# A hybrid decoder layer on one core: gate's second K half multiplied first for all feature tiles, stored, and added later

## The chip, the core and the metric

One core of one Trainium2 chip computes the whole layer. Its engines work side by side: TensorE (PE) multiplies, VectorE (DVE) and ScalarE (ACT) do elementwise work, GpSimd (POOL) a little, and SyncE (SP) issues most transfers. The metric is the device time of one execution in microseconds. Before the change it was 1936.91 us, the median of 3 runs (1934.86 to 1938.24).

## The reference, cut to what matters

```python
x = x + 0.5 * swiglu_ffn(rmsnorm(x, ffn1_norm), ffn1_w_gate, ffn1_w_up, ffn1_w_down)
x = x + hybrid_mixer(rmsnorm(x, mix_norm), ...)
x = x + 0.5 * swiglu_ffn(rmsnorm(x, ffn2_norm), ffn2_w_gate, ffn2_w_up, ffn2_w_down)
return rmsnorm(x, final_norm)

def rmsnorm(x, g):                       # scale of a token: 1 / rms over its 1024 features
    y = x * lax.rsqrt(jnp.mean(x * x, axis=-1, keepdims=True) + EPS)
    return y * g
def swiglu_ffn(x, w_gate, w_up, w_down):
    return (jax.nn.silu(x @ w_gate) * (x @ w_up)) @ w_down
```

x is 1024 tokens by 1024 features in float32; the feed-forward width is 2816. The change touches only the two feed-forward blocks, and there only gate and up. The mixer between them (attention and gated linear attention) stays as it is.

## The kernel before, in words

Tokens lie as columns, features on the partitions. Every float32 operand is split in two parts, a high one by a copy on ACT and a low one, the remainder, by a subtraction on DVE. A product of two such operands is three matmuls (`mm3`, L192 to L194): high by high, high by low, low by high, 128 x 128 weights against 512 tokens.

Gate and up of a feed-forward block are done for 22 feature tiles of 128 (FT = 22). Call gate's two K halves of a tile A11 and A12, up's A21 and A22, and the tokens' quarters B11, B21 (first and second K half of the first 512 tokens) and B12, B22 (the same of the second 512). A *product* is one weight half against one token quarter: four 128-row weight blocks, 12 matmuls. A *plain* tile takes 8 products (`plain`). A tile by the seven-product scheme (`strassen`) takes 7: A11 x B11, A12 x B21, S1 x T1, S2 x T2, S3 x T3, S4 x B22, A22 x T4, where S1 to S4 are sums of weight halves (`sums`, L396) and T1 to T4 differences of token quarters (`combine`, L333 for the differences and L312 for their low parts). T's are made once a block, S's once a tile. So T1 to T4 must be there before the first such tile, and in each block some plain tiles come first: 4 (`std, rms_of = 4, [None]`) in block 1, 2 in block 2.

Block 1 begins with tokens that have only their gain (`lift`, L319 and L320): the token scale is not known yet, and the plain tiles' results of the first 512 tokens are multiplied by it afterwards (`rb`, L510 and L513). Meanwhile side work (`first`) finds the scale (squares on ACT, sums on DVE, a matmul with ones L267, a power on POOL, a broadcast by matmul L279), scales the tokens in place (L303, L1877), splits and combines them.

The order of the work is written out: the recording code makes PE's products one after the other, and after every three matmuls a clock (`tick`) lets the side work take one step. The steps are counted: `until(24)` and `t0 + k == 28` are numbers of such steps. Weights are copied and split a few products ahead (`LOOK = 4`), each engine works through its own queue in order, and an instruction that waits holds everything behind it on its engine. A tile's raw weights come as two 512 KB transfers on SP's queue (`load`), gate's into one of three `raw` buffers.

After a tile of the seven-product scheme four steps collect its banks: p1 copies bank X after A11 x B11 and p2 adds A12 x B21's own bank Z to it (L564), which gives gate for the first 512 tokens; p6 and p5 copy X after S2 and S1 (L541), and p5's second step adds bank Y (L573); p3 takes gate for the second 512 tokens, p4 up. A22 x T4 is accumulated on bank Y, so it waits for p5's addition. X and Y alternate between two pairs of banks.

Of the kernel before, what the change touches and what calls it, by code (L numbers as in the profile page):

```python
# [32 lines left out]
AHEAD2 = 12  # L33


class Layer:
# [256 lines left out]
    def normed(self, rb, x, h, which, half, inplace=False, pace=1):  # L293
# [4 lines left out]
        for k in range(KT + 2):  # L298
            if k > 1:
                lows.pop(0)()  # L300
            if k < KT:
                hf = x[:, k, ts] if inplace else self.nt.tile([128, 512], F32, name="hf")
                nc.vector.scalar_tensor_tensor(hf, x[:, k, ts], self.gains[:, which, k:k + 1], rb,  # L303
                                               op0=OP.mult, op1=OP.mult)
                lows.append(self.halve(h[half][k], hf))
            for _ in range(int((k + 1) * pace) - int(k * pace)):
                yield
# [6 lines left out]
    def lift(self, x, h, which, half, k):  # L314
# [3 lines left out]
        hi = h[half][k][:, 0]  # L318
        nc.scalar.activation(hi, xk, AF.Copy, scale=gain)  # L319
        nc.vector.scalar_tensor_tensor(h[half][k][:, 1], xk, gain, hi.bitcast(F32), op0=OP.mult, op1=OP.subtract)  # L320
# [8 lines left out]
    def combine(self, x, B, std, pace=1):  # L329
# [20 lines left out]
        for name, k0, ts in (("T2", 4, hi), ("T3", 0, hi), ("T1", 0, lo), ("T4", 4, lo)):  # L350
            while self.room("TA") < (5 if self.pos[0] >= 8 * std - 2 else 9):
                self.reserve = 4 * (self.pos[0] >= 8 * std)
                if lows:
                    lows.pop(0)()
                yield
# [15 lines left out]
    def ffn(self, w, B, rb, std, late, load, raws, hooks):  # L371
# [9 lines left out]
        tb = self.dram.tile([HK, 128, 2, 512], F32, name="tb")  # L381
        minus = lambda o, p, q: nc.vector.tensor_tensor(o, p, q, OP.subtract)
# [14 lines left out]

        def source(f, q):
            if q[0] == "S":
# [4 lines left out]
        def ready(f, q, kinds):  # L404
# [3 lines left out]
            if q == "A12" and f >= std:  # L408
# [5 lines left out]
            def low():  # L414
                nc.vector.tensor_tensor(t[:, 1], a, t[:, 0].bitcast(F32), OP.subtract)  # L415
                if q == "A11" and f >= std:
                    sums(f, 1)
                if q in ("S1", "S4"):
# [30 lines left out]
        def both(i, banks, post):  # L449
# [10 lines left out]
            for m in range(2):  # L460
                q = f"A{m + 1}{i + 1}"
                seq.append(((0, q), lambda kinds, q=q: ready(0, q, kinds), mm if m else lambda: None, post if m else None))

# [79 lines left out]
        def strassen(f):  # L543

            def pair():
                if f not in X:
                    X[f], Y[f] = [self.one_bank((f - FT) % 2 * 2 + i) for i in range(2)]
                    partner(f)
                return X[f]
# [21 lines left out]
            def p5():  # L571
                snap(G[0][:, 1], X[f])
                todo.append([0, lambda: nc.vector.tensor_tensor(G[0][:, 1], Y[f], G[0][:, 1], OP.add)])  # L573
# [167 lines left out]
        groups = {f: strassen(f) for f in range(std, FT)}  # L741
        for f in range(std, FT):
# [3 lines left out]
            groups[f][2]()  # L746
# [31 lines left out]
        def step(i=None):  # L778
# [3 lines left out]
            if make and key not in made:  # L782
# [10 lines left out]
                if key[1] in ("A11", "A12"):  # L793
# [8 lines left out]
        def go():  # L802
            for i, (key, _, mm, post) in enumerate(seq):
# [20 lines left out]
                if i == turn - 1:  # L824
                    self.free(*G)
            self.free(*S, *s2.values())
        return step, settle, go


# [941 lines left out]
    def run(self, ffn=True):  # L1771
# [16 lines left out]
        h = [[self.take("AT", "h") for _ in range(KT)] for _ in range(2)]  # L1788
# [26 lines left out]
        load_x(0, 0, 1)  # L1815
        one(w1, 0, 0, 0)
        load_x(0, 1, 1)
        one(w1, 0, 1, 0)
        load_x(0, 2)
        one(w1, 0, 0, 1)  # L1820
        load_x(0, 4)
        one(w1, 0, 1, 1)
        load_x(0, 6, 1)
        load_x(0, 7, 1)
        for m in range(2):
            one(w1, 1, m)
        self.load_consts()
        for k in range(0, KT, 2):
            load_x(1, k)
        ns, B = [{}, {}], {f"u{i + 1}{half + 1}": h[half][4 * i:4 * i + 4] for i in range(2) for half in range(1)}  # L1830
# [5 lines left out]
        def begin(step, settle):  # L1836
            for k in range(KT):
                self.lift(x, h, 0, 0, k)
                if k in (0, 1, 3, 5):
# [3 lines left out]
        def first(std):  # L1843
# [9 lines left out]
            for half, t0 in enumerate((0, 24)):  # L1853
                yield from until(t0)
                if half:
                    for _ in range(2):
                        next(rms[0])
                for k in range(KT):
                    if half and t0 + k == 28:
                        for _ in range(2):  # L1860
                            next(rms[0])
                    self.squares(ns[half], x, slice(half * 512, half * 512 + 512), k, nc.vector, "hf" if half else "acc")
                    yield from until(t0 + k + 1)
                    if half and t0 + k == 30:
                        nc.scalar.activation(rb[:, 0], ns[0]["rb"], AF.Copy)
                self.total(ns[half], nc.vector)
            yield from until(36)
            for _ in range(2):
                next(rms[1])
            yield from until(40)  # L1870
            for _ in range(2):
                next(rms[1])
            yield from until(41)
            yield from self.normed(ns[1]["rb"], x, h, 0, 1, True, 2.5)
            B["12"], B["22"] = h[1][:4], h[1][4:]
            for k in range(KT):
                nc.vector.scalar_tensor_tensor(x[:, k, :512], x[:, k, :512], self.gains[:, 0, k:k + 1], rb[:, 0],  # L1877
                                               op0=OP.mult, op1=OP.mult)
                yield
            while self.pos[0] < 4 * std:  # L1880
                yield
            lows = []
            for k in range(KT + 2):
                if k > 1:
                    lows.pop(0)()
                if k < KT:
                    lows.append(self.halve(h[0][k], x[:, k, :512]))
                if k in (5, 9):
                    B["21" if k > 5 else "11"] = h[0][k - 5:k - 1]
                yield  # L1890
            yield from self.combine(x, B, std)
            while self.pos[0] < 8 * std:
                yield
# [33 lines left out]
        def again(src):  # L1927
# [9 lines left out]
            def back():  # L1937
# [5 lines left out]
        std, rms_of = 4, [None]  # L1943
        self.open_banks(False)
        step, settle, go = self.ffn(w1, B, lambda: rms_of[0][:, 0], std, 5, loader(w1), raws,
                                    {"post": post, "x": again(ins["xT"]), (10, "A22"): self.round_consts,
                                     ("2", 3, 2): lambda: self.raws(0), ("3", 0): lambda: self.later(2),
                                     (std, "A11"): lambda: self.free(*B.pop("12"), rms_of[0])})
# [4 lines left out]
        self.side.append(first(std))  # L1953
# [11 lines left out]
        B, std = {}, 2  # L1965
        out = {}

        def second(x):
            for half in range(2):
# [9 lines left out]
                B[f"1{half + 1}"], B[f"2{half + 1}"] = hg[half][:4], hg[half][4:]  # L1979
            yield from self.combine(x, B, std)  # L1980
# [57 lines left out]
        def post2(ts, ot):  # L2038
# [9 lines left out]
            if ot == (3 if half else 7):  # L2048
# [3 lines left out]
        step, settle, go = self.ffn(w2, B, lambda: None, std, 1, loader(w2), raws,  # L2052
                            {"post": post2, "x": again(xs), "parts": (slice(0, 256), slice(256, 512)), (std, "A11"): lambda: self.free(*B.pop("12"))})
        for half in range(2):
            ts = slice(half * 512, half * 512 + 512)
            for i in range(2 * half, KT + 2 * half):
# [15 lines left out]
                if half and ot == 5:  # L2072
                    loader(w2)(0)
# [128 lines left out]
```

## Time and profile before

| quantity | value |
|---|---|
| median of the runs | 1936.91 us |
| span of the profiled execution | 1938.6 us |
| granted PE clock, mean | 0.997 |
| PE busy | 1922.5 us (99%) |
| DVE, ACT busy | 1334.0 us (69%), 862.1 us (44%) |
| moved by DMA | 292.47 MB, 151 GB/s |
| first matmul of block 1's weights | 5.63 us |
| first T product of block 1, of block 2 | 105.33 us, 1338.93 us |
| first product of block 2 | 1287.61 us |

The page has no time for the profiled execution beside its span; that span lies 0.4 us above the slowest of the three runs. A row of the timeline gives start, duration, engine, line, operation, output and inputs, and in brackets how long the engine stood idle before and what it waited for. Matmul durations overlap, so the spacing of their starts is what one costs.

### The profile page before, as it was taken

Reading aid. Unit: us, or ns where it says so; the run is one execution under the profiler, and the core shown is the slowest. Engines: PE = TensorE matmul, PEld = TensorE weight load, DVE = VectorE, ACT = ScalarE, POOL = GpSimd, SP = SyncE. Lnnn points to the kernel's source line nnn. Section 1 sums busy time; section 2 is a strip of 40 time slices with the busy share of each in tenths; the row PEclk is TensorE's granted clock in tenths of the full one; section 3 lists DMA queues with packets and bytes.
Section 4 is the critical chain, followed back from the end, with each engine's and each line's share of the span. In section 5 each row is a group of like instructions: output and inputs, shape, how many; then the busy total and the mean of one; then the engine's idle time right before and its main releaser. Section 6 shows DMA issues by size and latency. Waiting matters only on the chain.

```text
span 1938.6 us, 26019 instructions
## 1 busy us (share of the span) xinstructions
PE 1922.5 (99%) x9363; PEld 1581.6 (82%) x9363; DVE 1334.0 (69%) x2234; ACT 862.1 (44%) x1653; POOL 219.1 (11%) x251
## 2 busy tenths in 40 slices
PE   9999999999999999999999999999999999999998
PEld 7888888888888888778877888888888888888887
DVE  7976667676776762454868887468666677667766
ACT  6343333334444551323479887234333333353443
POOL 0000000000000010121467654000000000000001
PEclk9999999999999999999989999999999999999999
DMA  7323244449874330118453522622323353488652
GB/s 263 114 76 115 96 160 142 157 151 346 299 260 152 111 102 26 55 44 250 135 154 94 146 73 90 231 104 82 114 77 125 109 180 133 162 319 290 228 182 88
DMA packets 155745, 292.47 MB, mean 151 GB/s; under 512 B 15744, under 2 KB 47104, under 8 KB 155296
## 3 DMA queue, kind: packets, MB, share of 16 engines
q1 hardware_dynamic: 147456, 275.83, 41.8%
q0 software_dynamic: 2304, 10.23, 1.6%
q10 hardware_dynamic: 5856, 4.75, 0.8%
q8 instruction: 74, 1.21, 0.3%
q14 instruction: 55, 0.45, 0.1%
HBM read 213.25 MB, written 81.85 MB: 152 GB/s over the span
## 4 chain that ended last, share of the span: by engine, by line
PE 94%; ACT 2%; DVE 2%; issue 1%; DMA 0%; POOL 0%; ACTq 0%; POOLq 0%; SPq 0%; DVEq 0%
PE bank L192 25%; PE bank L193 25%; PE bank L194 25%; PE pair L1342 3%; PE bank L1414 3%; PE bank L874 2%; PE bank L876 2%; PE bank L875 2%; PE bank L1432 1%; PE bank L1433 1%; ACT p L1383 1%; PE bank L1067 0%; PE pair L1350 0%; PE bank L992 0%; PE pair L983 0%
## 5 line engine op out<-in xcount | busy, mean ns | idle before, releaser
L192 PE MATMUL bank<-h,wt 128*128 128x512 f32 x648 | 254.0, 392 | 0.6 <-ACT wt L412 0.6
L194 PE MATMUL bank<-h,wt 128*128 128x512 f32 x648 | 252.7, 390 | 0.0
L193 PE MATMUL bank<-h,wt 128*128 128x512 f32 x648 | 252.6, 390 | 0.0
L192 PE MATMUL bank<-bd,wd 128*128 128x512 f32 (+1 forms) x632 | 243.0, 385 | 0.0
L194 PE MATMUL bank<-bd,wd 128*128 128x512 f32 (+1 forms) x632 | 242.5, 384 | 0.0
L193 PE MATMUL bank<-bd,wd 128*128 128x512 f32 (+1 forms) x632 | 242.5, 384 | 0.0
L194 PE MATMUL bank<-T,wt 128*128 128x512 f32 x608 | 236.6, 389 | 0.0
L192 PE MATMUL bank<-T,wt 128*128 128x512 f32 x608 | 236.6, 389 | 0.0
L193 PE MATMUL bank<-T,wt 128*128 128x512 f32 x608 | 236.6, 389 | 0.0
L274 POOL TENSOR_TENSOR r<-v,mhalf 128x4 f32<-128x4 f32 (+1 forms) x9 | 9.7, 1075 | 1348.6 <-DVE v L272 1348.6
L415 DVE TENSOR_TENSOR wt<-v,wt 128x512 fp32r<-128x512 f32 x152 | 103.9, 686 | 66.4 <-ACT wt L412 66.3
L192 PEld LDWEIGHTS bank<-h,wt 128*128 128x128 f32 x648 | 122.1, 188 | 27.0 <-ACT wt L412 1.5
L194 PEld LDWEIGHTS bank<-h,wt 128*128 128x128 f32 x648 | 121.9, 188 | 25.6 <-DVE wt L415 0.2
L193 PEld LDWEIGHTS bank<-h,wt 128*128 128x128 f32 x648 | 122.0, 188 | 25.0
L194 PEld LDWEIGHTS bank<-bd,wd 128*128 128x128 f32 x632 | 118.7, 188 | 23.6
L193 PEld LDWEIGHTS bank<-bd,wd 128*128 128x128 f32 x632 | 118.8, 188 | 23.3
L192 PEld LDWEIGHTS bank<-bd,wd 128*128 128x128 f32 x632 | 118.8, 188 | 23.2
L192 PEld LDWEIGHTS bank<-T,wt 128*128 128x128 f32 x608 | 114.1, 188 | 23.9
L193 PEld LDWEIGHTS bank<-T,wt 128*128 128x128 f32 x608 | 114.1, 188 | 23.7
L194 PEld LDWEIGHTS bank<-T,wt 128*128 128x128 f32 x608 | 114.1, 188 | 23.6
L541 ACT ACTIVATE g<-bank 128x512 f32<-128x512 f32 x76 | 45.4, 598 | 196.7 <-PE bank L194 196.7
L192 PE MATMUL bank<-h,w 128*128 128x512 f32 x320 | 127.3, 398 | 0.0
(290 smaller groups left out, 3891.7 us busy)
## 6 DMA issues: line engine op xcount, KB each, us to landing
in<-in_w_f_dram SPq DMA_DIRECT2D x132, 256.0 KB, 5.4
in<-b SPq DMA_DIRECT2D x132, 256.0 KB, 5.4
raw<-in_w_f_dram SPq DMA_DIRECT2D x43, 512.0 KB, 5.1
up<-in_w_f_dram SPq DMA_DIRECT2D x43, 512.0 KB, 5.5
raw<-in_w_in_dram SPq DMA_DIRECT2D x23, 512.0 KB, 3.8
b<-g SPq DMA_DIRECT2D x44, 256.0 KB, 2.0
l<-tb SPq DMA_DIRECT2D x22, 512.0 KB, 4.5
b<-l SPq DMA_DIRECT2D x44, 256.0 KB, 2.8
```

Of the source, the lines that this page charges most:

```text
L192: mm(ps, w[0], x[0], start=first, stop=False, skip_group_check=True)
L193: mm(ps, w[0], x[1], start=False, stop=False, skip_group_check=True)
L194: mm(ps, w[1], x[0], start=False, stop=last, skip_group_check=True)
L415: nc.vector.tensor_tensor(t[:, 1], a, t[:, 0].bitcast(F32), OP.subtract)
L541: nc.scalar.activation(dst, src, AF.Copy)
L874: mm(p, a, w[:, 0, c], start=f, stop=False, skip_group_check=True)
L875: mm(p, a, w[:, 1, c], start=False, stop=False, skip_group_check=True)
L876: mm(p, b, w[:, 0, c], start=False, stop=l, skip_group_check=True)
L1342: nc.tensor.matmul(s[:, i + c, :w], Q[:, j, r], kk[br, g][:, k0:k0 + w], start=(j == 0 and i % per == 0), stop=False, skip_group_check=True)
L1383: nc.scalar.activation(p[:, i].rearrange("p (c w) -> p c w", c=nch), sv[:, i * nch:i * nch + nch], AF.Exp, bias=nm[:, i:i + 1], accum_out= ...
L1414: nc.tensor.transpose(t[:, r * 128:r * 128 + 128], heads[r][:, k * 128:k * 128 + 128], self.ident)
L1432: mm(o, v, pt[:, 0], start=False, stop=False, skip_group_check=True)
```

## The change

Both blocks take all 22 tiles by the seven-product scheme, and no tile is plain (`std` is 0). In exchange, the product A12 x B21 of every tile is taken out of its tile and done at the beginning of the block, for all 22 tiles one after the other. It needs only a quarter of the tokens and none of the T's. Its bank is copied by ACT to one half of a two-half buffer (`kept`), sent to a DRAM tile (`pd`, 256 KB a tile), and reloaded (`recall`) when the tile's other products run; p2 then adds the buffer instead of bank Z. The weights A12 of a tile are loaded alone for this (`ahead`, two tiles in one raw buffer) and again with the rest of gate later.

In block 1 the early products use the first 512 tokens' second K half with the gain but without the token scale, in four tiles of their own. When such a product is added, DVE first multiplies it by the scale (`weigh`). The tokens' scaling, splitting and combining moves into the stretch of these 22 products: the steps of the scale's computation are now 18, 22, 25 and 29 (the dictionary `due`), where they were 24, 28, 36 and 40, and the pace of the rest is PACE = 1.35 steps. In block 2 the scaled tokens are used, the hold on weights moves from A11 of tile 1 to A12 of tile 4, and the second half of the tokens needs only its second K quarter split.

```diff
+        def ahead(j, parts=(0, 1)):
+            if j not in E:
+                E[j] = self.raw.tile([128, 1024], F32, name="raw", tag="raw")
+            for i in parts:
+                if 2 * j + i < D:
+                    nc.sync.dma_start(E[j][:, i * 512:i * 512 + 512], w[2 * j + i, 0, :, 512:])
+        def save(f):
+            def post():
+                t = kept()[:, f % 2]
+                snap(t, Z.pop(f))
+                send(pd[f], t)
+                if f == D - 1:
+                    recall(0)
+            return post
+        def recall(f):
+            if f < D:
+                send(kept()[:, f % 2], pd[f])
+        def weigh(f):
+            if f < D and rb() is not None:
+                t = kept()[:, f % 2]
+                nc.vector.tensor_tensor(t, t, rb(), OP.mult)
...
                     partner(f)
+                    recall(f + 1)
...
                 snap(st["a"], X[f])
+                if f < D:
+                    if f == 0:
+                        weigh(0)
+                    p2()
...
-                nc.vector.tensor_tensor(a, Z.pop(f), a, OP.add)
+                nc.vector.tensor_tensor(a, kept()[:, f % 2] if f < D else Z.pop(f), a, OP.add)
...
-                todo.append([0, lambda: nc.vector.tensor_tensor(G[0][:, 1], Y[f], G[0][:, 1], OP.add)])
+                def more():
+                    nc.vector.tensor_tensor(G[0][:, 1], Y[f], G[0][:, 1], OP.add)
+                    weigh(f + 1)
+                todo.append([0, more])
...
         groups = {f: strassen(f) for f in range(std, FT)}
+        if D:
+            begun = "begun" in hooks
+            if begun:
+                first2()
+            for f in range(2 * begun, D):
+                product(f, "A12", "21", lambda f=f: one(f), True, True, save(f))
         for f in range(std, FT):
             groups[f][1]()
             if f > std:
                 groups[f - 1][3]()
-            groups[f][2]()
+            if f >= D:
+                groups[f][2]()
...
+            due = {18: lambda: go_on(0), 22: lambda: go_on(0), 25: lambda: go_on(1), 29: lambda: go_on(1),
+                   23: lambda: nc.scalar.activation(rb[:, 0], ns[0]["rb"], AF.Copy)}
+            for n, (half, k) in enumerate([(0, k % KT) for k in range(4, 12)] + [(1, k) for k in range(KT)]):
...
-        std, rms_of = 4, [None]
+        step, settle, go = self.ffn(w1, B, lambda: rms_of[0][:, 0], 0, 5, loader(w1), raws, hooks1, FT)
...
-        B, std = {}, 2
+        step, settle, go = self.ffn(w2, B, lambda: None, 0, 1, loader(w2), raws, hooks2, late2)
```

The order of DVE's queue in block 1, where the second 512 tokens are scaled. First the kernel before: `wt` is a weight's split, `h` a token part's low part, `hf`, `sq` and `g` the plain tiles' gate and up.

```order
L415 TENSOR_TENSOR wt_566<-up_386,wt_566 128x512
L312 TENSOR_TENSOR h_211<-x_196,h_211 128x512
L312 TENSOR_TENSOR h_212<-x_196,h_212 128x512
L1877 SCALAR_TENSOR_TENSOR x_196<-x_196,gains_60,rb_307 128x512 x8
L510 TENSOR_TENSOR hf_695<-bank_493,rb_307 128x512
L513 TENSOR_TENSOR sq_696<-bank_494,rb_307 128x512
L514 SCALAR_TENSOR_TENSOR g_533<-g_533,hf_695 128x512
L515 TENSOR_TENSOR g_533<-g_533,sq_696 128x512
L312 TENSOR_TENSOR h_197<-x_196,h_197 128x512
```

The same engine and place with the change:

```order
L436 TENSOR_TENSOR wt_501<-raw_348,wt_501 128x512
L304 SCALAR_TENSOR_TENSOR x_196<-x_196,gains_60,bank_452 128x512 x2
L436 TENSOR_TENSOR wt_534<-raw_400,wt_534 128x512
L304 SCALAR_TENSOR_TENSOR x_196<-x_196,gains_60,bank_513 128x512 x3
L436 TENSOR_TENSOR wt_554<-raw_400,wt_554 128x512
```

The plain tiles' gate work (L510 to L515) has gone from between, and one weight split stands between every two or three token instructions.

DVE's queue in block 1 where the half products end and the seven-product tiles begin. With the change (`kept` is the buffer with the reloaded half product, `rb` the token scale, `T4` the last difference, `v` a weight sum):

```order
L436 TENSOR_TENSOR wt_852<-v_773,wt_852 128x512
L334 TENSOR_TENSOR x_196<-x_196 128x512 x3
L533 TENSOR_TENSOR kept_342<-kept_342,rb_296 128x512
L640 TENSOR_TENSOR hf_901<-kept_342,hf_901 128x512
L313 TENSOR_TENSOR T4_883<-x_196,T4_883 128x512
L334 TENSOR_TENSOR x_196<-x_196 128x512
L313 TENSOR_TENSOR T4_884<-x_196,T4_884 128x512
L642 SCALAR_TENSOR_TENSOR g_905<-g_905,hf_901 128x512
L436 TENSOR_TENSOR wt_875<-raw_822,wt_875 128x512
```

And in the kernel before, at T4:

```order
L564 TENSOR_TENSOR hf_1018<-bank_1020,hf_1018 128x512
L333 TENSOR_TENSOR x_196<-x_196 128x512 x3
L312 TENSOR_TENSOR T4_1046<-x_196,T4_1046 128x512
L566 SCALAR_TENSOR_TENSOR g_533<-g_533,hf_1018 128x512
L415 TENSOR_TENSOR wt_989<-v_896,wt_989 128x512
```

The addition to `hf` read a bank; it now reads `kept`, behind a multiplication of `kept`, and the split of the next weights (`wt_875`) stands behind both.

SP's queue around the same place, with the change:

```order
L546 DMA pd_224<-kept_342 128x512 x6
L1887 DMA raw_822<-in_w_f1_dram 128x1024
L1887 DMA up_824<-in_w_f1_dram 128x1024
L546 DMA pd_224<-kept_342 128x512 x2
L546 DMA kept_342<-pd_224 128x512 x2
L1887 DMA raw_995<-in_w_f1_dram 128x1024
```

And before, at the start of the stretch of plain tiles:

```order
L1797 DMA raw_487<-in_w_f1_dram 128x1024
L1797 DMA up_489<-in_w_f1_dram 128x1024
L475 DMA b1_244<-g_533 128x512 x3
L475 DMA l_703<-b1_244 128x512
L475 DMA b1_244<-g_533 128x512
```

The stores of the half products (`pd<-kept`) and their reloads (`kept<-pd`) have come between the weight loads; the first reload stands behind the last two stores. In all, SP issues 1011 transfers where it issued 888, and PE 8966 matmuls where it issued 9038.

More of the change, by code (lines that the diff above doesn't have):

```diff
@@ L1787, in run @@
         x = new_x()
-        h = [[self.take("AT", "h") for _ in range(KT)] for _ in range(2)]
+        half_of = lambda k0: [self.take("AT", "h") if k0 <= k < k0 + 4 else None for k in range(KT)]
+        h = [half_of(0), half_of(4), half_of(4)]
         raws = {}
@@ L1814, in run @@
         w1, w2 = ins["w_f1"], ins["w_f2"]
[L1815 to L1830, printed above, removed]
+        ns, B = [{}, {}], {"21": h[2][4:]}
         def to_slots():
@@ L1852, in first @@
             rb = rms_of[0] = self.take("TA", "rb", F32)
[L1853 to L1878, printed above, removed]
-                yield
@@ L1880, in first, with go_on @@
[L1880 to L1893, printed above, removed]
+            def go_on(half, n=2):
+                for _ in range(n):
+                    next(rms[half])
@@ new lines, in scaled @@
+            def scaled():
+                for half in range(2):
+                    while f"rb" not in ns[half]:
+                        yield
+                    yield from self.normed(ns[half]["rb"], x, h, 0, half, True, PACE)
+                    B[f"{half + 1}{half + 1}"] = h[half][4 * half:4 * half + 4]
+                yield from self.combine(x, B, FT, PACE)
+            rest = scaled()
+            while True:
+                yield
+                clock[0] += 1
+                if clock[0] in due:
+                    due.pop(clock[0])()
+                if clock[0] > 23:
+                    try:
+                        next(rest)
+                    except StopIteration:
+                        break
@@ L1941, in again @@
             return back
-        std, rms_of = 4, [None]
+        rms_of = [None]
         self.open_banks(False)
[L1945 to L1948, printed above, removed]
+        hooks1 = {"post": post, "x": again(ins["xT"]), (10, "A22"): self.round_consts, "begun": True,
+                  ("2", 3, 2): lambda: self.raws(0), ("3", 0): lambda: self.later(2),
+                  (FT - 1, "S1"): lambda: self.free(rms_of[0])}
+        step, settle, go = self.ffn(w1, B, lambda: rms_of[0][:, 0], 0, 5, loader(w1), raws, hooks1, FT)
+        ahead = hooks1["ahead"]
+        load_x(0, 4, 1)
+        ahead(0, (0,))
+        load_x(0, 5, 1)
+        ahead(0, (1,))
+        load_x(0, 6)
+        ahead(1)
+        load_x(0, 0)
+        load_x(0, 2)
+        ahead(2)
+        self.load_consts()
+        for k in range(0, KT, 2):
+            load_x(1, k)
         blank = self.one_bank(7)
@@ L1952, in run @@
         begin(step, settle)
-        self.side.append(first(std))
+        self.side.append(first())
         go()
@@ L2077, in run @@
             self.free(*h[half])
-            hg[half] = [self.take("AT" if half else "TA", "h") for _ in range(KT)]
+            hg[half] = [None] * 4 * half + [self.take("AT" if half else "TA", "h") for _ in range(KT - 4 * half)]
             if half == 0:
@@ L2081, in run @@
         self.unring()
-        loader(w2)(1)
-        self.hold = (1, "A11")
+        ahead(1)
+        ahead(2)
+        self.hold = (4, "A12")
         go()
```

94 lines of the change are left out of this document (74 added, 20 removed).

## The prediction

> **What bounds the kernel now.** I read the page's head first, then PE's waits in the two feed-forward blocks, then PE's own rows for the real cost of one matmul.
>
> ```profile
> span 1938.6 us, 26019 instructions
> PE 1922.5 (99%) x9363; PEld 1581.6 (82%) x9363; DVE 1334.0 (69%) x2234; ACT 862.1 (44%) x1653; POOL 219.1 (11%) x251
> PE 94%; ACT 2%; DVE 2%; issue 1%; DMA 0%; POOL 0%; ACTq 0%; POOLq 0%; SPq 0%; DVEq 0%
> PE bank L192 <- ACT wt L412: 0.6, 1, 0.6
> 300.00:400.00 100.00, 100.00 (x443) 82.81 (x442) 71.95 (x112) 35.48 (x63) 0.00 (x0) 1.00 0.46 160
> 1277.64 0.39 PE L193 MATMUL bank<-h,w 128*128 128x512 f32 x1
> ...
> 1287.61 0.39 PE L192 MATMUL bank<-h,wt 128*128 128x512 f32 x1
> ```
>
> PE (the chain's 94%) hardly ever waits: in the weight products of both blocks ("wt") its one wait is 0.6 us, at the start. So a matmul taken away is time taken away, if nothing else becomes late. Its price is not the duration: rows of 0.39 us overlap. Between the two PE rows lie 44 starts in 9.97 us, **0.2267 us each**; the stretch 300 to 400 us holds 443, which agrees. A product (4 weight blocks, three matmuls each, 12) is 2.72 us, not 4.7. The columns of the stretch are PE, weight loads, DVE, ACT, POOL, clock, DMA share: the clock is full, DVE has 28 us free in 100, ACT 65.
>
> **What the change removes.** A feature tile that was computed plainly took 8 products, one by the seven-product scheme takes 7. Block 1 had 4 plain tiles, block 2 had 2; now there are none: 6 products, 72 matmuls, 72 x 0.2267 = **16.3 us**. The instruction order says the same: 9038 matmuls before, 8966 now. The other matmuls only move.
>
> **What it adds, and what hides it.** For each of 44 tiles: ACT copies the bank to a buffer, SP stores 256 KB, later reloads them, and loads the second half of gate's weights once more (132 DMAs, 35 MB); in block 1 DVE multiplies the reloaded tile by the tokens' scale.
>
> ```profile
> 1385.46 0.60 ACT L541 ACTIVATE g<-bank 128x512 f32<-128x512 f32 x1 [2.04 <-PE bank L194]
> 1385.95 0.62 ACT L412 ACTIVATE wt<-v 128x512 fp32r<-128x512 f32 x1
> b<-g SPq DMA_DIRECT2D x44, 256.0 KB, 2.0
> b<-sq SPq DMA_DIRECT2D x22, 256.0 KB, 3.2
> l<-b SPq DMA_DIRECT2D x6, 256.0 KB, 2.8
> in<-b SPq DMA_DIRECT2D x132, 256.0 KB, 5.4
> ```
>
> A copy costs 0.60 us of ACT; with the product's weight copy (0.62) that is 1.2 us in 2.72, so ACT hides it. The copy waits for PE's product and the next weight copy stands behind it, but weights are prepared some four products ahead (10.9 us), and PE would see this only if that lead were gone: then 1.2 us a product, 53 us in all. The buffer has two halves, so a store must have landed before the copy two products later (5.44 us): 0.6 + 2.0 to 3.2 = 2.6 to 3.8 us. At 0.46 of the DMA's share, 35 MB more are hidden too. Cost of these: 0.
>
> **DVE in block 1 is the tight place.** Until now 32 plain products covered the scaling, splitting and combining of the tokens; now 22 half products and one more do. I count DVE's instructions in the new order, from the first scaled token to the addition that the first A22 x T4 product waits for, and price them by rows of the same work, as spacing:
>
> ```profile
> 54.91 5.39 DVE L1877 SCALAR_TENSOR_TENSOR x<-x,gains,rb 128x512 f32<-128x512 f32 x8
> 62.94 4.90 DVE L312 TENSOR_TENSOR h<-x,h 128x512 fp32r<-128x512 f32 x8
> 67.75 4.79 DVE L333 TENSOR_TENSOR x<-x 128x512 f32<-128x512 f32 x7
> 86.60 0.69 DVE L396 TENSOR_TENSOR v<-up 128x512 f32<-128x512 f32 x1
> 87.32 0.69 DVE L396 TENSOR_TENSOR v<-v,raw 128x512 f32<-128x512 f32 x1
> 87.93 0.68 DVE L396 TENSOR_TENSOR v<-raw,up 128x512 f32<-128x512 f32 x1
> ```
>
> One that needs the one before starts 0.72 us after it (86.60 to 87.32), one that does not 0.61. 16 scalings x 0.67 = 10.8; 16 differences x 0.68 = 10.9; 24 low parts x 0.61 = 14.7; 20 weight splits x 0.61 = 12.2; 8 weight sums x 0.64 = 5.1; 5 others 2.7. Together **56.4 us** (89 instructions). The time for it comes from PE:
>
> ```profile
> 5.63 0.79 PE L192 MATMUL bank<-h,wt 128*128 128x512 f32 x1 [0.59 <-ACT wt L412]
> 26.10 0.94 PE L267 MATMUL bank<-ones,acc 128*128 128x1 f32 x8
> 29.77 1.05 PE L279 MATMUL bank<-ident,r 128*128 128x128 f32 x8
> 105.33 0.39 PE L192 MATMUL bank<-T,wt 128*128 128x512 f32 x1
> ```
>
> The first T product was the 35th, at 105.3; now it is the 24th: 105.3 - 11 x 2.72 = 75.4. A22 x T4 stands five products later, 89.0. The token scale's broadcast stood at step 28 of the side work (29.8 us); it moves to step 22, six steps of three matmuls earlier: 25.7, done at 26.7. So 62.3 us are there, 5.9 more than the work. DVE then waits twice in its own queue: for the second half's sums (step 25: 25.7 + 1.0 + 2.0 + 0.9 = 29.6, less one scaling done meanwhile: 2.2 us), and for the first reload. At that instruction 17 others (10.6 us) are still to come, so DVE is there at 26.7 + 45.8 + 2.2 = 74.7. The last A12 product ends at 72.7; copy, issue of its store (0.4, as SP's rows) and the reload's 2.8 give 76.8. DVE stands 2.1 us, and everything behind it: the split of the next A11 weights, T4's low parts, the addition. It ends at 76.8 + 10.6 = 87.4 against 89.0: **in time by 1.6 us**. By the other row for a reload (5.4 instead of 2.8) it is 1.0 late; with DVE at 0.69 an instruction, 3.4 late (61.4 + 4.3 - 62.3). Bounds 0 and 3.4; a gain is excluded, since PE does not wait there today. I take **0.5**, near the low end, because the spacing rows are the same instructions.
>
> A rule speaks against that choice. The Trainium skill, "VectorE: DVE Perf Modes", section "The DRAIN you can't avoid", says that the next operation does not start before the pipe is empty, so each would cost its full duration. Here eight splits of 0.69 us ran in 4.90 us, so the trace agrees only for dependent ones (0.72); by the rule the sum would be 3.4 late instead of 0.5.
>
> **The rest of the seven-product groups.** A group shrinks from 7 products (19.04 us, between the outer rows) to 6 in sequence, 16.3.
>
> ```profile
> 1367.05 0.69 DVE L573 TENSOR_TENSOR g<-bank,g 128x512 f32<-128x512 f32 x1 [1.78 <-ACT g L541]
> 1370.29 0.69 DVE L415 TENSOR_TENSOR wt<-v,wt 128x512 fp32r<-128x512 f32 x1 [1.95 <-ACT wt L412]
> 1372.49 0.69 DVE L581 SCALAR_TENSOR_TENSOR acc<-acc,bank 128x512 f32<-128x512 f32 x1 [1.51 <-ACT acc L578]
> 1386.09 0.69 DVE L573 TENSOR_TENSOR g<-bank,g 128x512 f32<-128x512 f32 x1 [1.71 <-ACT g L541]
> ```
>
> DVE does 18 to 21 instructions in it, at 0.61 to 0.72 at most 15 us, under 16.3. The waits in its rows end on PE and ACT and so move with PE. The addition before A22 loses a product of distance: two products (5.44 us) instead of three; copy and addition take 1.3 us (1385.46 to 1386.78) after the bank is full. In block 2 the half products need only the first half's tokens, and the second half gets 22 products of cover where 8 stood. Cost: 0; without this cover each of 40 groups could lose up to 2.7.
>
> **Sum.** -16.3 + 0.5 = -15.8. Against the profiled execution, whose span is 1938.6 (the page shows nothing around it): 1922.8. That span is 1.7 over the median of the three runs, 1936.9; on the median: **1921.1**.
>
> **Rivals.** *A, the forecast*: 1919 to 1924. *B, DVE late at the hand-over of block 1*: it runs at 0.69 an instruction (3.4), with or without the slow reload (2.6 more): 1924 to 1927. For it: DVE is the only engine with under 6 us in hand; against it: the 4.90 us row. *C, the stall drops PE's clock.* PE began at half pace:
>
> ```profile
> 9.01 0.43 PE bank L192
> 9.44 0.43 PE bank L193
> 9.86 0.43 PE bank L194
> 10.29 0.27 PE bank L192
> ```
>
> From 5.63 to 10.29 each matmul took 0.43 us, so a PE that has stood still may lose half of 4.7 us once more: B plus 2.3, 1926 to 1929. No wait of this trace's matmuls between 10 us and the mixer was long enough to show it. The Trainium skill, "TensorE: Matmul & The Clock Gate", section "Part 1: The HAM clock gate", gives about 3.4 us of idleness for that; the starting rows agree with its half rate, no run here shows its threshold. *D, slower, by the stores of the half products*: both buffer halves wait for their store, ACT's copy waits, and with it every weight copy behind, so PE goes at the stores' pace. A pair of products then takes 0.6 + 0.4 + the landing; from 4.4 us on it exceeds 5.44, and over 22 pairs it eats 16.3 us from 5.2 on. If the stores landed like the queued loads of weights (6.4 for 512 KB):
>
> ```profile
> in<-in_w_f_dram SPq DMA_DIRECT2D x22, 512.0 KB, 6.4
> ```
>
> 7.4 - 5.44 = 2.0 us a pair, 43 us: 1936.9 - 16.3 + 43 = 1964. Against it: no store row of 256 KB is over 3.2. *E, no change*: the same, with landings near 5.2, or several small waits of 12 to 20 us in sum: 1933 to 1941.
>
> **How the numbers follow.** A 0.71, B 0.14, C 0.04, D 0.06, E 0.05. A measurement of this kernel tells 0.2% (3.9 us) from nothing. Faster is A + B + C, 0.89; same 0.05; slower 0.06. The range runs from the full 16.3 us plus two of spread in the runs (1918.5) to the end of C, 1929; it leaves out D and E.
>
> **What would show it.** Right: PE has 8966 matmuls, 0.2267 apart; the first T product starts near 75.4; PE's waits in the weight products stay under 4 us in sum; the half products' stores land in 2 to 3.2 us; the down products of both blocks are unchanged. Wrong: PE rows that wait for DVE's "wt", T4 or the "g" addition between 75 and 95 us (B); rows of 0.43 us behind them (C); ACT copies of "kept" that wait for a DMA, every second product (D); PE waiting once a group for "wt" in both blocks (a group that does not fit 16.3 us), which would cost most.

## The result: 1946.3 us, slower by half a per cent

| | median | range | runs |
|---|---|---|---|
| before | 1936.5 us | 1934.9 to 1938.2 | 4 |
| changed | 1946.3 us | 1945.1 to 1947.4 | 4 |

Changed over before is 1.0052, with a 95% interval of 1.0040 to 1.0064. The prediction was 1921.1 us, in a range of 1918.5 to 1929: wrong in sign, by 25 us. A run's time is its span plus 1.8 us in the records of these runs, so the changed kernel's profiled execution (span 1944.2) stands for its median. The profile of before does not: its span of 1938.6 is 4 us above what its median implies. A second profile of before, told of below, is used where stages are subtracted.

**The profile after.** The page's head, the share of the chain, and PE's waits, longest first, of the changed kernel:

```profile
span 1944.2 us, 26337 instructions
PE 1909.6 (98%) x9291; PEld 1569.5 (81%) x9291; DVE 1370.5 (70%) x2292; ACT 898.1 (46%) x1717; POOL 219.8 (11%) x251
PE 88%; DVE 4%; ACT 3%; DMA 3%; issue 1%; POOL 1%; SPq 0%; ACTq 0%; POOLq 0%; DVEq 0%
PE bank L193 <- ACT hf L612: 6.6, 2, 5.9
PE bank L280 <- POOL r L275: 5.5, 3, 4.9
PE bank L268 <- DVE acc L257: 4.0, 2, 3.4
```

PE holds 88% of the chain instead of 94%, and has three waits that before did not have: 5.9, 4.9 and 3.4 us. Where they are is told by PE's count of matmuls in equal stretches (columns: length, then PE, weight loads, DVE, ACT, POOL busy with their counts, clock, DMA share, GB/s). First before, then after:

```profile
0.00:100.00 100.00, 98.39 (x431) 78.53 (x432) 80.22 (x129) 46.62 (x80) 3.82 (x8) 1.00 0.53 185
```

```profile
0.00:100.00 100.00, 86.76 (x365) 67.41 (x366) 73.27 (x120) 58.03 (x104) 3.95 (x8) 0.95 0.68 235
100.00:200.00 100.00, 100.00 (x443) 82.82 (x442) 75.12 (x117) 38.10 (x67) 0.00 (x0) 1.00 0.38 132
...
1270.00:1305.00 35.00, 31.57 (x134) 26.35 (x133) 12.86 (x22) 8.35 (x15) 1.40 (x1) 0.90 0.38 124
```

In block 1's first 100 us there are 66 matmuls fewer (15 us of PE), and the granted clock is 0.95. From 100 us on PE is as dense as before, 443 per 100 us, up to the mixer: the groups of six products fit. The other thin stretch, clock 0.90, is the start of block 2.

**First place, block 1's broadcast of the token scale.** The timeline of the changed kernel, all engines mixed; a bracket is the idle time just before and what ended it:

```profile
21.66 1.05 PE L268 MATMUL bank<-ones,acc 128*128 128x1 f32 x8 [0.57 <-DVE acc L257]
...
28.03 0.69 DVE L252 TENSOR_TENSOR hf<-hf,sq 128x512 f32<-128x512 f32 x1 [0.22 <-ACT sq L248]
28.64 0.15 DVE L273 TENSOR_SCALAR v<-bank 128x4 f32<-128x4 f32 x1
...
28.87 1.52 POOL L275 TENSOR_TENSOR r<-v,mhalf 128x4 f32<-128x4 f32 x1 [28.44 <-DVE v L273]
...
30.45 1.72 PE L280 MATMUL bank<-ident,r 128*128 128x128 f32 x8 [4.88 <-POOL r L275]
```

PE's sums are done at 22.6. The small instruction `v` that reads them stands on DVE behind five additions of the second half's squares, and three of these wait for ACT's squares (1.2 us at most). It runs six microseconds late, the power takes 1.5 more, and PE stands 4.88 us.

**Second place, the first T product.** ACT's rows of the changed kernel, then PE's:

```profile
41.79 0.62 ACT L433 ACTIVATE wt<-raw 128x512 fp32r<-128x512 f32 x1
52.79 0.60 ACT L612 ACTIVATE kept<-bank 128x512 f32<-128x512 f32 x1 [10.37 <-DMA pd<-kept]
...
86.76 1.23 ACT L312 ACTIVATE T<-x 128x512 fp32r<-128x512 f32 x2 [0.25 <-DVE x L334]
87.90 0.58 ACT L612 ACTIVATE hf<-bank 128x512 f32<-128x512 f32 x1
```

```profile
88.53 0.79 PE L193 MATMUL bank<-T,wt 128*128 128x512 f32 x1 [5.93 <-ACT hf L612]
89.12 0.63 PE L194 MATMUL bank<-T,wt 128*128 128x512 f32 x1
...
92.11 0.50 PE L195 MATMUL bank<-T,wt 128*128 128x512 f32 x1
92.44 0.39 PE L193 MATMUL bank<-T,wt 128*128 128x512 f32 x1
```

At 42.4 ACT stops for 10.37 us: the next copy of a half product wants a buffer half whose store has not landed. Forty microseconds later PE wants a bank that ACT's copy `hf` must empty first; the copy stands behind T's copies, which wait for DVE, which is late. After the wait rows start 0.43 us apart until 92.1. What held the store is in the DMA view of the stretch from 37 to 53 us of the changed kernel (queue: packets, MB, share of 16 engines; then issues with KB and median us to landing):

```profile
q0 software_dynamic: 96, 4.19, 76.0%
q1 hardware_dynamic: 541, 0.98, 16.5%
pd<-kept SPq DMA_DIRECT2D x2, 256.0 KB, 12.3
qx<-in_c_qx_dram POOLq DMA_DIRECT2D x1, 9.1
```

GpSimd copies two of the mixer's constants, 4.2 MB, in just these microseconds, and two half products' stores take 12.3 us. The kernel before has the same transfers at the same time, and shows in the same stretch what they do to a store:

```profile
q0 software_dynamic: 93, 4.19, 76.1%
b<-g SPq DMA_DIRECT2D x2, 256.0 KB, 9.9
```

**Third place, the start of block 2.** SP's, ACT's, DVE's and PE's rows of the changed kernel:

```profile
1280.45 1.30 SPq L407 DMA_DIRECT2D raw<-in_w_f_dram  x2
1290.86 0.38 SPq L2158 DMA_DIRECT2D xs<-x  x1
1291.33 2.27 SPq L407 DMA_DIRECT2D raw<-in_w_f_dram  x4
...
1295.61 1.28 ACT L433 ACTIVATE wt<-raw 128x512 fp32r<-128x512 f32 x2 [4.05 <-DMA raw<-in_w_f_dram]
...
1296.27 0.69 DVE L436 TENSOR_TENSOR wt<-raw,wt 128x512 fp32r<-128x512 f32 x1 [4.83 <-ACT wt L433]
1296.88 0.68 DVE L257 TENSOR_TENSOR acc<-acc,sq 128x512 f32<-128x512 f32 x1
...
1297.62 1.87 PE L268 MATMUL bank<-ones,acc 128*128 128x1 f32 x8 [3.43 <-DVE acc L257]
```

The changed code asks for gate's halves of tiles 0 and 1, then (when those are split) for 6 and 7 at 1280.5, and only after the mixer's last token store for 2 to 5, at 1291.3. ACT waits 4.05 us for tile 2's, DVE's split waits for ACT, the last addition of the squares waits behind the split, and PE's sums wait 3.43 us for it.

### The profile page after: what moved, and what is told of

Same layout as the page of the kernel before. It is cut to its first block, busy times and chain, and to the rows that moved or that the text cites. A ratio compares the mean times of both kernels' runs of the same rounds, so it can differ in the third digit from the quotient of the medians.

```text
span 1944.2 us, 26337 instructions
## 1 busy us (share of the span) xinstructions
PE 1909.6 (98%) x9291; PEld 1569.5 (81%) x9291; DVE 1370.5 (70%) x2292; ACT 898.1 (46%) x1717; POOL 219.8 (11%) x251
## 4 chain that ended last, share of the span: by engine, by line
PE 88%; DVE 4%; ACT 3%; DMA 3%; issue 1%; POOL 1%; SPq 0%; ACTq 0%; POOLq 0%; DVEq 0%
PE bank L193 23%; PE bank L194 23%; PE bank L195 23%; PE pair L1431 3%; PE bank L1503 3%; PE bank L963 2%; PE bank L965 2%; PE bank L964 2%; PE bank L1521 1%; PE bank L1522 1%; DMA raw<-in_w_f_dram 1%; ACT p L1472 1%; DMA pd<-kept 1%; PE bank L1156 0%; PE pair L1439 0%
## 5 line engine op out<-in xcount | busy, mean ns | idle before, releaser
L193 PE MATMUL bank<-T,wt 128*128 128x512 f32 x704 | 275.0, 391 | 7.0 <-ACT hf L612 6.6
L194 PE MATMUL bank<-T,wt 128*128 128x512 f32 x704 | 274.6, 390 | 0.0
L195 PE MATMUL bank<-T,wt 128*128 128x512 f32 x704 | 274.5, 390 | 0.0
L193 PE MATMUL bank<-h,wt 128*128 128x512 f32 x528 | 208.0, 394 | 0.5 <-ACT wt L433 0.5
L195 PE MATMUL bank<-h,wt 128*128 128x512 f32 x528 | 206.7, 392 | 0.4 <-DVE wt L436 0.3
L194 PE MATMUL bank<-h,wt 128*128 128x512 f32 x528 | 206.7, 391 | 0.0
L275 POOL TENSOR_TENSOR r<-v,mhalf 128x4 f32<-128x4 f32 (+1 forms) x9 | 10.4, 1159 | 1355.2 <-DVE v L273 1355.2
L612 ACT ACTIVATE g<-bank 128x512 f32<-128x512 f32 x88 | 52.7, 598 | 236.3 <-PE bank L195 236.3
L193 PEld LDWEIGHTS bank<-T,wt 128*128 128x128 f32 x704 | 132.6, 188 | 35.7 <-ACT hf L612 7.5
L195 PEld LDWEIGHTS bank<-T,wt 128*128 128x128 f32 x704 | 132.6, 188 | 27.6
L194 PEld LDWEIGHTS bank<-T,wt 128*128 128x128 f32 x704 | 132.6, 188 | 27.6
L433 ACT ACTIVATE wt<-v 128x512 fp32r<-128x512 f32 x176 | 109.9, 624 | 76.7 <-PE bank L195 50.9
L193 PE MATMUL bank<-h,w 128*128 128x512 f32 x320 | 127.2, 398 | 0.0
L195 PE MATMUL bank<-h,w 128*128 128x512 f32 x320 | 124.9, 390 | 0.0
L436 DVE TENSOR_TENSOR wt<-v,wt 128x512 fp32r<-128x512 f32 x176 | 120.6, 685 | 6.0 <-ACT wt L433 5.6
L194 PE MATMUL bank<-h,w 128*128 128x512 f32 x320 | 124.7, 390 | 0.0
```

The source lines that it names most:

```text
L193: mm(ps, w[0], x[0], start=first, stop=False, skip_group_check=True)
L194: mm(ps, w[0], x[1], start=False, stop=False, skip_group_check=True)
L195: mm(ps, w[1], x[0], start=False, stop=last, skip_group_check=True)
L433: nc.scalar.activation(t[:, 0], a, AF.Copy)
L612: nc.scalar.activation(dst, src, AF.Copy)
```

## The experiments

Each is the changed kernel with the edit shown; in some of them the line numbers are two higher (L614 for L612). Before was run beside each on the same chip, with medians of 1936.0 to 1936.1 us.

**1. The mixer's constants later.**

```diff
-    def round_consts(self):
+    def round_consts(self, late):
+        t = self.small.tile([128, 4], F32, name="r")
+        self.nc.gpsimd.tensor_tensor(t, late, self.mhalf, OP.mult)
...
-                  (10, "A22"): self.round_consts,
+                  (10, "A22"): lambda: self.round_consts(raws[11][0][:, :4]),
```

> Edit: the changed kernel, but GpSimd's two loads of the mixer's constants (4.2 MB, issued at 37 us, right under the stores of the half products) first wait for a weight tile that arrives near 250 us. Theory S (the stores hold ACT): the store issued at 41.9 us landed only 10.4 us later because it shared the DMA engines with these 4.2 MB; ACT's copy of the next half product waited for it, the weight copies stood behind it, DVE's weight splits behind those (6.9 us), and so the sums of the token blocks and the copy before the first T product came late. Without the two loads ACT's longest wait for a store in block 1 falls under 4 us, DVE's 6.9 us wait goes, PE's wait of 5.93 us at the first T product and the nine half-rate rows behind it (1.9 us) go: 1946.3 - 7.8 = 1938.5 us (1937 to 1941). Theory V (DVE has too much work, whatever the stores do): ACT's wait goes, but PE's wait at the first T product stays within 2 us of 5.9: 1944 to 1947.

Measured: **1938.45 us** (1936.4 to 1939.7), 1.0011 [1.0002, 1.0019] of before. ACT's waits for a store between 10 and 83 us, first in the changed kernel and then here, and the first T product here:

```profile
ACT kept L612 <- DMA pd<-kept: 16.2, 5, 10.4
DVE wt L436 <- ACT wt L433: 9.3, 2, 6.9
```

```profile
ACT kept L614 <- DMA pd<-kept: 0.2, 1, 0.2
DVE wt L438 <- ACT wt L435: 2.6, 1, 2.6
PE bank L195 <- ACT hf L614: 0.7, 1, 0.7
```

Theory S holds at every link: 16.2 us of ACT's waits become 0.2, DVE's 9.3 become 2.6, and PE's 5.93 become 0.7.

**2. Four halves instead of two for the half products,** with the constants where they were.

```diff
             if not H:
-                H.append(self.take("TA", "kept", F32))
-            return H[0]
+                H.extend(self.take("TA", "kept", F32) for _ in range(2))
+            return H[f // 2 % 2][:, f % 2]
```

> Edit: the changed kernel with a buffer of four halves for the half products instead of two (one slot of 4 KB a partition more); the constants still come at 37 us. A store may now land within four products (10.9 us) instead of two. Theory S (stores that land late and a buffer of two halves together hold ACT): in the run with the constants late the wait at the first T product had shrunk from 5.93 to 0.7 us; the same follows here, since a landing of 12 us costs ACT only 1 to 2 us instead of 10.4: PE's wait at the first T product under 1.5 us, 1938 to 1940.5 us. Rival (the constants take the DMA engines from the weights too, and the weights are what ACT lacks): ACT waits for weight loads instead, PE's wait stays over 4 us, 1944 to 1947.

Measured: **1938.95 us** (1936.3 to 1940.1), 1.0013 [1.0004, 1.0021].

```profile
ACT kept L612 <- DMA pd<-kept: 2.6, 1, 2.6
PE bank L193 <- ACT hf L612: 0.8, 1, 0.8
```

The same 7 us are won from the other side. The stores beside the 4.2 MB still took 11.1 us in the median, and ACT waited no longer for weight loads (2.3 us) than in the changed kernel (2.7), so the rival is out. Neither the 4.2 MB nor the buffer of two halves is enough by itself: the stall needs a landing longer than the buffer's two products.

**3. Block 2's loads in order of use.**

```diff
                 if half and ot in (7, 0):
+                    ahead(2 if ot == 0 else 1)
                     step()
...
-        ahead(1)
-        ahead(2)
         self.hold = (4, "A12")
```

> Edit: in block 2 the second and third pair of gate halves are loaded before the fourth pair (behind the token stores of tiles 7 and 0 of the mixer's last product), not after it. Theory L (the order of the loads): at 1290 us ACT waits 4.05 us for a weight load that SP issued at 1291.3, behind the fourth pair's; DVE's split waits behind ACT, the last sum of the squares behind the split, PE's sums behind that (3.43 us), and half-rate rows follow until 1304. With the loads in order of use ACT's wait and PE's 3.43 us go, and with them some 3 us of half rate: 1946.3 - 6.2 = 1940.1 us (1938.5 to 1942). Rival (DVE's sum is late because the last token tile comes from PE only at 1290.1, whatever the loads do): PE still waits over 2 us for the sums, 1944 to 1947.

Measured: **1940.18 us** (1939.5 to 1943.4), 1.0023 [1.0013, 1.0033]. SP's and PE's rows here:

```profile
1281.05 7.74 SPq L407 DMA_DIRECT2D raw<-in_w_f_dram  x6
1294.62 0.95 PE L268 MATMUL bank<-ones,acc 128*128 128x1 f32 x8
```

All six loads go out from 1281, the sums wait for nothing, and no half-rate row follows. The last token tile is added no sooner (1290.7 us against 1290.2 in the changed kernel), so the rival is out.

**4. The broadcast later in PE's order, alone.**

```diff
-            due = {18: lambda: go_on(0), 22: lambda: go_on(0), ...
-                   23: lambda: nc.scalar.activation(rb[:, 0], ns[0]["rb"], AF.Copy)}
+            due = {18: lambda: go_on(0), 30: lambda: go_on(0), ...
+                   31: lambda: nc.scalar.activation(rb[:, 0], ns[0]["rb"], AF.Copy)}
...
-                if clock[0] > 23:
+                if clock[0] > 31:
```

> Edit: block 1's broadcast of the token scale moves from step 22 of the side work to step 30 (8 x 0.68 = 5.4 us more of PE work before it), with all that follows it; nothing else. Theory S (DVE's start, not PE's, sets the hand-over): the wait of 4.88 us at the broadcast goes, but the power is ready no sooner (30.4 us), DVE begins to scale no sooner, and the first T product is no sooner: the wait there grows from 5.9 to 10 us or more; what is saved is at most the half-rate rows (2 us): 1943.5 to 1947 us. Rival P (each wait of PE is lost by itself): the 4.88 us and the slow rows behind it (1.8 us) are won, the wait at the first T product stays 6 us: 1939.6 us (1938 to 1941.5).

Measured: **1945.7 us** (1942.4 to 1947.9), 1.0047 [1.0033, 1.0061]. PE's waits in block 1:

```profile
PE bank L193 <- ACT hf L612: 7.5, 1, 7.5
PE bank L268 <- DVE hf L257: 2.7, 1, 2.7
```

The wait at the broadcast is gone and the time is not. Theory S was right on the time and not on the place: of the 4.9 us 1.6 came back at the first T product (5.9 to 7.5), where 4 were expected, and 2.7 at a place that neither theory named, the second half's sums at step 25, which now came ahead of the broadcast.

**5. The second half's squares behind the first half's sums,** with the constants late.

```diff
-            for n, (half, k) in enumerate([(0, k % KT) for k in range(4, 12)] + [(1, k) for k in range(KT)]):
-                t = n if n < 8 else 10 + (n - 8) * 5 // 4
+            when = {19 + k * 3 // 2: k for k in range(KT)}      # second half's tile k at this step
+            for n, (half, k) in enumerate([(0, k % KT) for k in range(4, 12)]):
+                t = n
...
-                   25: lambda: go_on(1), 29: lambda: go_on(1)
+                   31: lambda: go_on(1), 35: lambda: go_on(1)
```

> Edit: as the run with the constants late, and the second half's squares (8 on ACT, 8 additions on DVE) are issued behind the first half's sums (steps 19 to 29, its own sums at step 31) instead of ahead of them (steps 10 to 18). Theory Q (the queue order): v stands on DVE behind five additions that wait for ACT's squares; ahead of them it runs right behind PE's sums (about 22.8 us), the power ends near 24.4, the broadcast at step 22 (25.6 us) does not wait, and the 4.88 us and the slow rows behind it (1.8 us) go. Against it DVE gets 8 additions (5.0 us) more to do between the broadcast and the hand-over, where it had 5.9 us in hand by the prediction's count. If both hold: 1938.5 - 6.7 = 1931.8 us (1930 to 1935). Theory V (DVE has no room there): the wait at the broadcast goes, and PE waits 4 to 7 us at the first T products instead: 1936 to 1940.

Measured: **1942.6 us** (1940.7 to 1943.9), against 1938.45 without this edit. Both theories missed it. PE's waits here:

```profile
PE bank L270 <- DVE hf L259: 7.0, 1, 7.0
PE bank L282 <- POOL r L277: 0.9, 1, 0.9
```

The queue order was the cause of the wait at the broadcast (4.85 to 0.9 us). But ACT's squares now stand behind a copy of a half product that waits 2.7 us for its store, DVE stands 4.16 us for them, and the additions then alternate with the scalings, so that the second half's sums make PE wait 7.0 us. That stall is the same work one place later, as in run 4.

**6. Dummy matmuls in the two waits of block 1.**

```diff
-            due = {18: lambda: go_on(0), 22: lambda: go_on(0), ...
+            due = {18: lambda: go_on(0), 22: lambda: (self.warm(blank, 18), go_on(0)), ...
...
+                  (0, "S2"): lambda: self.warm(self.one_bank(7), 22),
```

> Edit: the changed kernel with matmuls of zeros in the two long waits of block 1: 18 of 128x512 right ahead of the broadcast and 22 right ahead of the first T product; 4.1 and 5.0 us of PE work at 0.2267 us each, where PE stood 4.88 and 5.93 us. Theory C (standing still lowers the clock): no wait is shorter at its end, the broadcast and the first T product start where they did, but the rows behind them are 0.2267 us apart at once instead of 0.43: 1.6 us behind the first wait (the slower broadcast, 0.56, among it) and 1.9 behind the second, 1946.3 - 3.5 = 1942.8 us (1941.5 to 1944.5). Rival (the slow rows come from what feeds PE behind a wait, not from its clock): the rows stay 0.43 apart, 1946 to 1948.

Measured: **1942.6 us** (1940.0 to 1946.4), 1.0035 [1.0022, 1.0048].

```profile
25.34 4.06 PE L100 MATMUL bank<-blank 128*128 128x512 bf16 x18
30.37 1.16 PE L280 MATMUL bank<-ident,r 128*128 128x128 f32 x8 [0.97 <-POOL r L275]
31.28 0.48 PE L193 MATMUL bank<-h,wt 128*128 128x512 f32 x1
31.60 0.39 PE L194 MATMUL bank<-h,wt 128*128 128x512 f32 x1
```

The broadcast starts where it did (30.37 against 30.45), yet it takes 0.91 us to the next matmul instead of 1.37, and the rows behind it are 0.32 and then 0.23 us apart; behind the second wait it is the same. What feeds PE is as before, so the slow rows come from PE having stood still. The profiled execution is the slowest of the five. Its block 1 is 3.05 us shorter than the changed kernel's, near theory C's 3.5; its mixer is 3.8 us longer.

**7. Constants late and loads in order, together** (the edits of 1 and 3).

> Edit: the constants late (block 1) and the loads of the gate halves in order of use (block 2), together. Theory: the two losses lie in different blocks and add: 1938.45 - 6.1 = 1932.3 us (1931 to 1934), faster than the kernel before by 3.7. What is left against the predicted 1921.1 is then the wait of 4.85 us at block 1's broadcast with the slow rows behind it (2.5), DVE's last sum (1.1) and small rests. Rival (the mixer or block 2's down products give part of it back): 1934.5 or more.

Measured: **1932.9 us** (1930.8 to 1934.1), 0.9983 [0.9974, 0.9992] of before: the two losses add, and the version is faster than before by 0.17%.

**8. That, and block 1's scales later:** the first half's broadcast at step 30, the second half's sums and broadcast at 33 and 37 (in run 4 they had stayed at 25 and 29).

> Edit: as the run with both mended, and the token scales' steps of block 1 later: the first half's broadcast at step 30 instead of 22, the second half's sums and broadcast at steps 33 and 37 instead of 25 and 29. With the stores landing in time DVE has some room at the hand-over. Theory M (the room is more than the 5 us that PE gains): the wait of 4.85 us and its slow rows (2.5 us) go and nothing comes back at the first T product: 1932.3 - 6.5 = 1925.8 us (1924.5 to 1928). Theory S as before (DVE's start sets the hand-over): DVE begins to scale at 31 us as before, so the wait comes back at the T products, less the slow rows: 1929.5 to 1932.5.

Measured: **1927.4 us** (1926.8 to 1928.9), 0.9958 [0.9946, 0.9971]. The first T product here:

```profile
77.32 0.50 PE L195 MATMUL bank<-T,wt 128*128 128x512 f32 x1 [1.72 <-ACT hf L614]
```

With the stores out of the way the same move of the broadcast wins 5.5 us where it won nothing in run 4: theory M, less the 1.7 us that return here.

**9. Four halves on top of that.**

> Edit: as the run with the constants late, the loads in order and the scales' steps later (1927.4 us), with four halves for the half products instead of two. Theory S: ACT waited 2.9 us in sum for stores there, and PE 1.7 us at the first T product; with four halves ACT waits for no store, the first T product's wait falls under 1 us: 1926 us (1924.5 to 1927.2). Rival: that wait is DVE's and ACT's work, not a store's, and the time stays: 1927.2 to 1928.5.

Measured: **1926.1 us** (1925.4 to 1930.8), 0.9954 [0.9940, 0.9968]. The time lies in theory S's range, but the interval overlaps that of run 8. ACT waits for no store any more, and yet the wait that should have shrunk did not:

```profile
PE bank L195 <- ACT hf L614: 1.7, 1, 1.7
```

So by the trace the rival is right on the wait: it is a T copy of ACT's ahead of `hf`, which waits 0.81 us for DVE's differences, and no store. Where the 1.3 us between the two medians come from is not shown.

**10. The kernel before, profiled once more.**

> Edit: none; the kernel before once more, for a second profile. Its profiled execution had a span of 1938.6 us, while the other executions of it have 1933 to 1935 (their times less the 1.8 us that lie around a span). Theory M (the mixer varies): the feed-forward blocks take what they took (block 1 to its last sums 627.7 us, block 2 611.1), and the mixer between them takes 655 to 657 instead of 659.95; the changed kernels' mixers took 658.0 to 662.1, so about 2 to 3 us of the change's loss would lie there. Rival: a span of 1938 again, that is, the profile itself costs it: then the mixer loses nothing by the change, and the differences of the medians are to be read from the blocks alone.

Measured: one time, 1937.1 us; span 1935.3. Starts of the same instructions, this profile against the changed kernel's, give the change stage by stage:

| stage | before | changed | difference | predicted |
|---|---|---|---|---|
| block 1, to its last sums | 626.75 | 631.71 | +4.96 | -10.9 + 0.5 |
| mixer, to block 2's first weight product | 657.57 | 658.24 | +0.67 | 0 |
| block 2, to its last sums | 611.06 | 613.39 | +2.33 | -5.4 |
| rest | 39.92 | 40.86 | +0.94 | 0 |

In the first profile of before the same two blocks took 627.66 and 611.05 us, and its mixer 659.95. So the first profile's extra time lies mostly in the mixer, which the change does not touch, as theory M has it; but the mixer took more than its 655 to 657, and its part of the loss is 0.67 us, not 2 to 3. Over all twelve profiles told of here it took between 657.6 and 662.1 us, and the 0.67 is within that. Block 1 lost 15.8 us against the bare saving, block 2 7.8.

## Why the prediction was wrong

**Right.** A matmul is 0.2267 us (443 in 100 us), and six products' groups fit: the stretches from 100 us on have no wait of PE. The 16.3 us are there; in run 9, with the stalls mended, the kernel is 10 us faster than before. The wait at the hand-over, taken as 0.5 us between bounds of 0 and 3.4, was 1.7 in runs 8 and 9, within its bounds. Its place was another: the sum looked for it at A22 x T4, where PE waits for DVE's addition in none of these traces, and it came at the first T product (77.3 us where 75.4 was predicted), behind ACT's copy `hf`. The reloads landed in 5.7 us in the median, like the other row (5.4) and not the 2.8 of the sum; DVE waits 2.4 us for the first of them, and PE does not wait behind it. Two sums are off by 0.1 and 0.3 us (16 x 0.67 is 10.7, and the reload's terms come to 76.5), which changes nothing.

**Step that failed, 1: "it moves to step 22, six steps of three matmuls earlier: 25.7, done at 26.7".** This took only PE's order. What the broadcast needs, DVE's `v` and GpSimd's power, was not followed through their own queues. It started at 30.45. Cost, from the starts of PE's rows: 5.0 us of gap, 0.6 for a broadcast at half rate, 1.2 for the rows behind it.

**Step that failed, 2: "Cost of these: 0" for copies and stores.** Two errors. The landing was bounded by 2.0 to 3.2 us, medians over 44 and 22 stores, though the trace of before, asked for the microseconds in which the change would store, shows 9.9. And the lead of four products was checked for PE alone: "PE would see this only if that lead were gone". PE's weights did last through ACT's 10.4 us, but DVE has no lead. It lost 6.9 us there, more than the 5.9 that lay between its work and its time in the prediction's count (1.6 after the two waits that it allowed for), and came to the hand-over late. Cost: 6.1 us of gap and 1.9 of slow rows; runs 1 and 2 won 7.8 and 7.3 us back.

**Step that failed, 3: "Cost: 0" for block 2,** where only the need for tokens was looked at, not when the weights of the half products are loaded. The code shows it: the split of tile 1 calls `ahead(3)`, and that is emitted ahead of the line `ahead(1)`. Cost in the rows: 3.6 us of gap and 2.9 of half rate (sums 0.9, rows 1.3, broadcast 0.7); run 3 won 6.1 us back.

The three places come to 14.8 us of the 15.8 that block 1 lost, and to 6.5 of block 2's 7.8.

**The rivals.** D named the right mechanism, a copy held by its store, with a weight copy behind it, but made it a steady state of 22 pairs (43 us), and dismissed it by the medians. It was a few waits, one of them of 10.4 us out of 16.2, and that was enough, because B's tight engine stood behind it. The two were held to be separate cases; the loss needed both. C had the mechanism right (run 6), and its price of 2.3 us was the right size (1.8, 1.9 and 2.9 us), but it was tied to one stall of DVE's. There were three stalls, none of them in the sum. The Trainium skill, "TensorE: Matmul & The Clock Gate", section "Part 1: The HAM clock gate", puts the threshold near 3.4 us of idleness. Waits of 3.43, 4.88 and 5.93 us agree with it; the 2.69 us below and the rows of the mixer do not.

**What stays open.** Run 9 is 5 us above the predicted 1921.1. Against the second profile of before, its profile stands 2.3 us above the forecast in block 1, 0.7 in the mixer, 0.8 in block 2 and 0.4 in the rest; no run takes these away one by one.

## What to carry to other kernels

When an edit moves the start of a chain forward, follow every link of the chain through the queue of its own engine, and count what stands ahead of it there; PE's order says only when PE would be ready. Before a transfer is costed at nothing, ask the trace what else is on the DMA engines in just those microseconds: a median over the whole kernel hides the two that matter. And cover is had by an engine, not by a kernel: a lead that lets PE ride out a stall of ACT's does nothing for DVE, and a mended stall shows up at the next place (runs 4 and 5) until all of them are mended.

## What the runs showed of the hardware that was not expected

**A stall of PE costs more than its length, and 2.69 us of it were enough.** In the feed-forward blocks waits of 0.97, 1.25 and 1.72 us were followed by rows at full rate. A wait of 2.69 us (run 4) was followed by half rate from 30.65 to 37.2 us:

```profile
30.65 1.84 PE L268 MATMUL bank<-ones,hf 128*128 128x1 f32 x8 [2.69 <-DVE hf L257]
32.35 0.77 PE L193 MATMUL bank<-h,wt 128*128 128x512 f32 x1
...
37.19 0.49 PE L195 MATMUL bank<-h,wt 128*128 128x512 f32 x1
```

The half rate lasted 3.6 us after 5.93, 3.7 after 4.88, 6.5 after 2.69 and 7.0 after 7.0 (run 5), so its length does not follow the wait's. The dummies of run 6 prevented it in both waits. The length of one wait is not all that counts: in the mixer of before PE's longest wait between 960 and 1000 us is 0.8 us, and yet its rows go at half rate from 987 to 993 us, and the granted clock of the stretch (third number from the end) is 0.91:

```profile
960.00:1000.00 40.00, 38.45 (x287) 35.22 (x286) 26.21 (x53) 24.74 (x81) 19.47 (x31) 0.91 0.53 162
```

In the second profile of before it is 0.96 in the same stretch. What else decides it no run here shows.

**A bulk copy on one queue holds a small store on another.** Beside 4.2 MB from GpSimd's queue stores of 256 KB took 12.3 us (median of two); with that copy away, the stores of the same stretch took 2.1:

```profile
pd<-kept SPq DMA_DIRECT2D x5, 256.0 KB, 2.1
```

The Trainium skill, "DMA: Bandwidth & Descriptors", section "Queues, rings and completion order", says that each DMA engine goes round the queues packet by packet. The view of 37 to 53 us points the same way without proving it: packets of 44 KB on GpSimd's queue (4.19 MB in 96) against 1.8 KB on SP's (0.98 MB in 541), with shares of 76.0% and 16.5%.
